# A hybrid mixer layer: another order inside its last stage, four units moved into it, and its check moved to the end

## The chip, the cores and the metric

One core of a Trainium2 chip. The metric is device time in microseconds (us) of one execution of the whole layer, median of several runs. Changes of less than about 0.2% (2.7 us) can't be told from no change here.

## What is computed

One layer over 2048 tokens of width 1024: a conditioned norm of x, a wide projection (1024 to 3600 columns), three mixers on its columns, and an output projection with a residual and a last norm. Everything is in float32; the kernel gets float32 accuracy from TensorE by splitting operands in a high and a low part and summing three products.

```python
h = rms_norm(x) * (1.0 + scale) + shift          # scale, shift, gate from c @ w_ada + b_ada
p = h @ w_in                                     # columns: qa ka va lra ga | qb fb ib gb | qc kc vc gc
log_alpha = log_sigmoid(lra @ w_gla_gate2 + b_gla_gate) / 16
o_a = chunk_gated_linear_attn(qa / 8, ka, va, log_alpha)       # "GLA", 4 heads of 64/128, chunks of 64
log_f = logaddexp(log(lb), log1p(-lb) + log_sigmoid(fb))
o_b = chunk_gated_linear_attn(silu(qb), (1 - lb) * sigmoid(-fb), ib, log_f)   # "HGRN", 4 heads of 64/64
o_c = stick_breaking_attn(qc, kc, vc)            # 4 heads of 64, causal, blocks of 128
o   = [rms_norm(o_a) * gla_norm_w * silu(ga), rms_norm(o_b) * hgrn_norm_w * silu(gb), o_c * silu(gc)]
out = rms_norm(x + gate * (o @ w_out)) * final_norm_w
```

## The kernel before, in words

**Products.** A product in high and low parts is three matmuls (`mm3`, L263 to L266; lines 160 to 162 in `fm_unit`). A **projection unit** (`fm_unit`) makes one block of 128 feature columns for one stretch of 512 tokens: 8 times `mm3`, 24 matmuls of 128x512, summed in one of two PSUM banks (tag `acc` of pool `psA`). Its result leaves by an evacuation on ScalarE (ACT), `ev_act` at L191 or `ev_silu` at L826, and is stored to DRAM. Its weights are loaded and split by `split_w` (L146 load on SP, L147 high part on ACT, L148 low part on VectorE, DVE), in pool `wp` with two buffers each for `wraw`, `whi`, `wlo`. Results pass through pool `stg`, tag `st`, three buffers. Stretches of tokens are taken in the order 3, 2, 1, 0 (`ORDER`); the normed input of a stretch lies in SBUF as `hT[n]` (high and low).

**Stages.** First the norm, the conditioning and the first projections (to about 250 us), then the value columns in token-major units, then eight units for the HGRN forget gate whose evacuation (`ev_forget`, `decay_sums`, L533 to L554, L651 to L661) is a chain over ACT, DVE and GpSimd (POOL). Behind it stands the **flag** (L671 to L686): DVE takes minima of the decay sums in `SM`, TensorE adds up two columns over the partitions (`pf`, L682, in a bank of `psA`), and DVE makes the integer `fi`. At the end of the program `values_load` (L1512) reads it, and a branch runs an exact recurrence, which these inputs don't take. Then comes the **attention stage** (about 475 to 970 us): 80 steps of stick-breaking attention (`sb_stream`) interleaved with 50 projection units (`fill_stream`, `NFILL`), of which five are put ahead (`lead`). In these stages the compiler's list scheduler sets the order of each engine's queue from a simulated time line; each engine's queue is in order.

**Joint stage** (from 970 us, `recurrences_and_projection`). Here the order on TensorE (PE), DVE, ACT and POOL is the program's, written out by hand; SP, which issues the loads and stores, is still ordered by the scheduler. There are 16 steps i: four groups g of 512 tokens, in each the feature pairs 0, 2, 1, 3 (`STEPS`; 0 and 1 are GLA, 2 and 3 HGRN, so odd steps are HGRN). A step does:

- `scores` (PE, L1110) into a pair of banks (tag `two`, two pairs), `causal` (ACT copies them to M, L1116; POOL masks M, L1119)
- `square_sums` of the step before (PE, L1211), from the squares that `evacuate` made on ACT
- `keys` (PE transposes, L1126; ACT copy, L1128), `increments` (PE, L1138, into a pair of banks U), `states` (eight DVE steps in a row, L1147), `decays` of the next step (ACT exponentials, DVE products L1084 to L1092, one POOL product L1091)
- `outputs(i, 1)` and `outputs(i, 0)` (PE, L1168, L1179, into a pair of banks o). Between the two stands an **ordering detour**: PE writes one number (`done`, L1172), ACT copies it (`mark`, L1174), and PE multiplies the mark (L1164) before it goes on
- `evacuate` (ACT copies o to `ots`, L1196, and squares it, L1199; DVE multiplies by norm weight and gate, L1200)
- in odd steps one `attention_block` (k = 6 in steps 1, 5, 9, 13, k = 7 in steps 3, 7, 11, 15): load of the attention's result and gate, DVE product (L1218), ACT high part (L1223), DVE low part (L1224)
- every fourth step, for the group before: `norms` (ACT L1230, L1231; DVE L1233, L1234) and six times `normalise`: PE spreads a row (`bc`, L1238, one bank), DVE multiplies (L1239), ACT high part, DVE low part.

The high and low parts of the finished output go into the SBUF tiles of hT[3] and hT[2], by parity of the group. From step 5 on each step also holds 16 **pieces** `Y` of the output projection (a piece is one `mm3`, L1285 to L1287; eight pieces make half a row tile of 128 tokens, after which DVE adds x, L1290), placed 2+4+2+2+2+3+1 within the step. After the second half `finish` squares on ACT (L1253) and, some pieces later, DVE and POOL make the scale (L77, L78), DVE applies it (L1259) and SP stores. The 64 pieces of the last group follow the last step.

```python
            Y(2, on)
            nrm()
            if i < n:
                if i % 4 == 1:
                    attention_block(i // 4, 6)
                if i % 4 == 3:
                    attention_block(i // 4, 7)
                outputs(i, 1)
            nrm()
            Y(3, on)
            nrm()
            if i < n:
                outputs(i, 0)
                evacuate(i)
            Y(1, on)
```

## Time and profile before

| | us |
|---|---|
| median of 3 runs | 1350.9 (1350.4 to 1352.8) |
| the profiled execution | 1349.0 |
| its span in the trace | 1347.3 |
| PE busy | 1236.2 (92% of the span) |
| DVE, ACT, POOL busy | 677.1, 442.9, 160.2 |
| attention stage, lead units included | about 445 to 970 |
| joint stage | about 970 to 1347 |

The page divides the span in 40 slices of 33.7 us and gives each engine's busy share in tenths, and the TensorE clock that was granted in tenths of full speed. A line of the time line gives start and length of an instruction, and in brackets how long its engine had been idle and what ended that. A line of windows gives, for a stretch, each engine's busy time and instructions, the granted clock, the DMA share and GB/s.

### The profile page before, as it was taken

How to read it: one execution, taken by the hardware profiler on the slowest of the kernel's cores; microseconds unless marked ns; L12 is line 12 of the kernel's file. 1: busy time of each engine (PE TensorE's matmuls, PEld its weight loads, DVE VectorE, ACT ScalarE, POOL GpSimd, SP SyncE). 2: the span in 40 equal slices, each digit the busy share in tenths (PEclk: the TensorE clock that was granted, in tenths of full speed). 3: DMA queues.
4: the chain of work that ended last, by engine and by line, in shares of the span. 5: the costliest groups of instructions: out<-in, count | busy, mean ns of one | idle time of the engine just before them, and what ended most of it. 6: DMA issues, size and time to landing. Idle time of an engine off the chain costs nothing.

```text
span 1347.3 us, 22831 instructions
## 1 busy us (share of the span) xinstructions
PE 1236.2 (92%) x9322; PEld 1001.5 (74%) x9322; DVE 677.1 (50%) x1083; ACT 442.9 (33%) x830; POOL 160.2 (12%) x190
## 2 busy tenths in 40 slices
PE   7999999999994799999999999999775998989996
PEld 6777799999983677777777777777653776767675
DVE  5856316410059473465545665666346445564442
ACT  3375414321144242332333332332233323233211
POOL 3210000000024100100010112111121011111000
PEclk8999999999997899999999999999967799999999
DMA  9775433431134423232242234232354343543221
GB/s 263 223 260 165 148 93 106 138 109 48 55 106 146 133 59 81 89 94 59 81 116 76 74 105 132 83 88 67 101 178 121 93 159 116 154 145 123 75 87 56
DMA packets 153515, 155.17 MB, mean 115 GB/s; under 512 B 30117, under 2 KB 114102, under 8 KB 153402
## 3 DMA queue, kind: packets, MB, share of 16 engines
q1 hardware_dynamic: 124374, 116.39, 29.5%
q10 hardware_dynamic: 29028, 37.24, 7.9%
q8 instruction: 75, 1.23, 0.4%
q14 instruction: 38, 0.31, 0.1%
HBM read 101.16 MB, written 52.43 MB: 114 GB/s over the span
## 4 chain that ended last, share of the span: by engine, by line
PE 71%; DVE 14%; DMA 5%; issue 5%; ACT 4%; SPq 1%; POOL 1%; ACTq 0%; POOLq 0%; DVEq 0%
PE acc L160 8%; PE acc L162 8%; PE acc L161 8%; PE av L788 6%; PE acc L172 5%; PE acc L174 5%; PE acc L173 5%; PE pt L776 4%; PE y L1285 4%; PE y L1286 3%; PE y L1287 3%; PE o L1179 2%; PE o L1168 2%; DMA wg<-in_w_ada_dram 2%; PE acc L266 2%
## 5 line engine op out<-in xcount | busy, mean ns | idle before, releaser
L160 PE MATMUL acc<-hTh,whi 128*128 128x512 f32 x528 | 213.1, 405 | 1.5 <-DVE stl L285 1.0
L162 PE MATMUL acc<-hTh,wlo 128*128 128x512 f32 x528 | 210.0, 398 | 0.0
L161 PE MATMUL acc<-hTl,whi 128*128 128x512 f32 x528 | 208.4, 395 | 0.0
L772 DVE TENSOR_TENSOR_SCAN f<-f 128x512 f32<-128x512 f32 (+3 forms) x160 | 177.0, 1136 | 14.0 <-ACT f L766 6.9
L172 PE MATMUL acc<-whi,hTh 128*128 128x256 f32 (+1 forms) x512 | 146.2, 286 | 1.4 <-ACT stt L199 1.4
L174 PE MATMUL acc<-whi,hTl 128*128 128x256 f32 (+1 forms) x512 | 146.0, 285 | 0.0
L173 PE MATMUL acc<-wlo,hTh 128*128 128x256 f32 (+1 forms) x512 | 145.7, 285 | 0.0
L160 PEld LDWEIGHTS acc<-hTh,whi 128*128 128x128 f32 x528 | 99.9, 189 | 26.2 <-issue 5.1
L162 PEld LDWEIGHTS acc<-hTh,wlo 128*128 128x128 f32 x528 | 99.8, 189 | 23.3 <-issue 2.9
L161 PEld LDWEIGHTS acc<-hTl,whi 128*128 128x128 f32 x528 | 100.0, 189 | 20.0 <-issue 1.4
L1285 PE MATMUL y<-wh,hTh 128*128 128x512 f32 x256 | 108.6, 424 | 0.0
L1286 PE MATMUL y<-wl,hTh 128*128 128x512 f32 x256 | 101.7, 397 | 0.0
L1287 PE MATMUL y<-wh,hTl 128*128 128x512 f32 x256 | 101.3, 396 | 0.0
L766 ACT ACTIVATE f<-zt 128x512 f32<-128x512 f32 (+3 forms) x160 | 81.0, 537 | 58.1 <-DVE f L772 27.2
L172 PEld LDWEIGHTS acc<-whi,hTh 128*128 128x128 f32 x512 | 97.8, 191 | 1.8 <-ACT stt L199 1.6
L173 PEld LDWEIGHTS acc<-wlo,hTh 128*128 128x128 f32 x512 | 97.9, 191 | 0.2
L174 PEld LDWEIGHTS acc<-whi,hTl 128*128 128x128 f32 x512 | 97.8, 191 | 0.0
L788 PE MATMUL av<-PT,V 128*64 128x128 f32 x960 | 90.1, 280 | 1.3 <-DVE PT L781 1.2
L781 DVE COPY PT<-pt 128x512 f32<-128x512 f32 (+1 forms) x80 | 50.3, 628 | 73.5 <-PE pt L776 73.2
L148 DVE TENSOR_TENSOR wlo<-wraw,whi 128x1024 fp32r<-128x1024 f32 (+1 forms) x32 | 39.2, 1229 | 94.4 <-ACT whi L147 82.2
L776 PE MATMUL pt<-ident,f 128*128 128x128 f32 x544 | 84.6, 279 | 1.8 <-DVE f L772 1.4
L788 PEld LDWEIGHTS av<-PT,V 128*64 128x64 f32 x960 | 63.7, 136 | 28.5 <-issue 19.3
(210 smaller groups left out, 1963.0 us busy)
## 6 DMA issues: line engine op xcount, KB each, us to landing
wraw<-in_w_in_dram SPq DMA_DIRECT2D x36, 512.0 KB, 4.8
xt<-in_x_dram SPq DMA_DIRECT2D x16, 512.0 KB, 5.8
wa<-in_w_ada_dram SPq DMA_DIRECT2D x16, 512.0 KB, 6.0
Q<-s_qc SPq DMA_DIRECT2D x64, 128.0 KB, 3.2
s_gate<-sg ACTq DMA_DIRECT2D x32, 256.0 KB, 3.3
gt<-s_gate SPq DMA_DIRECT2D x32, 256.0 KB, 3.9
r<-in_x_dram SPq DMA_DIRECT2D x16, 512.0 KB, 3.6
out_dram<-r SPq DMA_DIRECT2D x16, 512.0 KB, 3.2
```

The costliest lines, as they stand in the source:

```text
L160: mm(ps, hi[:, k, :], th[:, k, :], start=(k == 0), stop=False)
L161: mm(ps, hi[:, k, :], tl[:, k, :], start=False, stop=False)
L162: mm(ps, lo[:, k, :], th[:, k, :], start=False, stop=(k == KT - 1))
L172: mm(o, th[:, k, s], hi[:, k, 0:ncols], start=(k == 0), stop=False)
L173: mm(o, th[:, k, s], lo[:, k, 0:ncols], start=False, stop=False)
L174: mm(o, tl[:, k, s], hi[:, k, 0:ncols], start=False, stop=(k == KT - 1))
L772: nc.vector.tensor_tensor_scan(fr, fr, fr, carry[u], op0=ALU.mult, op1=ALU.bypass)
L776: nc.tensor.transpose(pt[:, b, :], f[:, b * P:(b + 1) * P], ident)
L788: last[0] = mm(av[u * 64:(u + 1) * 64, :], (Dd if diag else V)[J][:, b, :], PT[:, b, :], start=diag, stop=(J == 0 and b == 0))
L1285: mm(y, oh[:, k, us], wh, start=(i == 0), stop=False)
L1286: mm(y, oh[:, k, us], wl, start=False, stop=False)
L1287: mm(y, ol[:, k, us], wh, start=False, stop=(i == KT - 1))
```

## The change

Seven edits. (1) The flag's instructions go into the joint stage as `flag()`, called after the last step's pieces; `pf` now takes a bank of tag `bc`, and `fi` is returned. (2) Four projection units leave the attention stage: of QA, KA and KA+P only two stretches each are made there (before 3, 3 and 4), `NFILL` is 46, and the four units become 32 pieces in steps 0 to 3 of the joint stage (8 ahead of step 0, then 6 a step, `SLOT0`). (3) Within a step `outputs(i, 1)` moves ahead of `keys`; the pieces stand in four stretches (4, 2, 6, 4); the detour (`done`, `mark`) is gone. (4) Both attention blocks come in steps 1, 5, 9, 13. (5) The low parts of `normalise` are made on POOL. (6) Homes: `wp` and `stg` live on through the joint stage; row tiles r use `wraw`/`whi` (four buffers, loaded three ahead), `fnb` and `bsel` use `wlo`; gates, attention results and the squares' junk share `stg`'s three `st` buffers; `ot` has six buffers instead of eight. (7) `finish` makes the scale on ACT (Ln, Exp) right behind the squares, the store follows after five pieces, and the very last row tile is scaled and stored in two halves.

```diff
-NFILL = 50
+NFILL = 46
+SLOT = (4, 2, 6, 4)
+SLOT0 = (2, 1, 2, 1)
...
-    def open_proj_pools():
-        nonlocal psA, wp, stg
-        psA = stA.enter_context(tc.tile_pool(name="psA", bufs=2, space=PSUM))
-        wp = stA.enter_context(tc.tile_pool(name="wp", bufs=2))
-        stg = stA.enter_context(tc.tile_pool(name="stg", bufs=3))
+    psA = stA.enter_context(tc.tile_pool(name="psA", bufs=2, space=PSUM))
+    wp = ctx.enter_context(tc.tile_pool(name="wp", bufs=2, reuse_waits="tile"))
+    stg = ctx.enter_context(tc.tile_pool(name="stg", bufs=3, reuse_waits="tile"))
...
-    pf = psA.tile([1, 2], F32, tag="acc", name="pf")
-    mm(pf, one_col, fl, start=True, stop=True)
...
-    feat_blocks.append((C_QA, ORDER[1:], ev_act((s_feat["qa"][0], AF.Copy, 1.0))))
-    feat_blocks.append((C_KA, ORDER[1:], ev_act((s_feat["ka"][0], AF.Copy, 1.0))))
-    feat_blocks.append((C_KA + P, ORDER, ev_act((s_feat["ka"][1], AF.Copy, 1.0))))
+    feat_blocks.append((C_QA, ORDER[2:], ev_act((s_feat["qa"][0], AF.Copy, 1.0))))
+    feat_blocks.append((C_KA, ORDER[2:], ev_act((s_feat["ka"][0], AF.Copy, 1.0))))
+    feat_blocks.append((C_KA + P, ORDER[2:], ev_act((s_feat["ka"][1], AF.Copy, 1.0))))
...
+    ka1 = split_w(C_KA + P, wp, P, P)
+    qa0 = split_w(C_QA, wp, P, P)
+    left = [(ka1, ORDER[0], ev["ka1"]), (ka1, ORDER[1], ev["ka1"]), (qa0, ORDER[1], ev["qa0"]),
+            (None, ORDER[1], ev["ka0"])]
...
-            else:
-                done = psG.tile([1, 1], F32, tag="sp", name="done")
-                mm(done, t.mark, t.mark, start=True, stop=True)
...
-            if e == 1:
-                done = psG.tile([1, 1], F32, tag="sp", name="done")
-                mm(done, one_col, one_col, start=True, stop=True)
-                t.mark = gq.tile([1, 1], F32, tag="mark", name="mark", bufs=2)
-                nc.scalar.copy(t.mark, done)
-            else:
+            if e == 0:
...
+            pf = psG.tile([1, 2], F32, tag="bc", name="pf")
+            mm(pf, one_col, fl, start=True, stop=True)
...
-            gt = po.tile([P, GTF], F32, tag="gt", name="gt", bufs=2)
+            gt = stg.tile([P, GTF], F32, tag="st", name="gt")
...
-            ots[k] = po.tile([P, GTF], F32, tag="ot", name="ot", bufs=8)
-            nc.sync.dma_start(ots[k], s_o[k][:, g * GTF:(g + 1) * GTF])
-            nc.vector.tensor_tensor(ots[k], ots[k], load_gate(g, k), op=ALU.mult)
-            split_ops(g, k)
+            ot, gt = stg.tile([P, GTF], F32, tag="st", name="oa"), load_gate(g, k)
+            nc.sync.dma_start(ot, s_o[k][:, g * GTF:(g + 1) * GTF])
+            nc.vector.tensor_tensor(ot, ot, gt, op=ALU.mult)
+            split_ops(g, k, ot, nc.vector)
...
-            split_ops(g, k)
+            split_ops(g, k, ots[k], nc.gpsimd)
...
+            nc.scalar.activation(f, f, AF.Ln, bias=eps_col, scale=1.0 / D)
+            nc.scalar.activation(f, f, AF.Exp, scale=-0.5)
...
-            r = pr_.tile([P, D], F32, tag="r", name="r", bufs=3)
+            r = wp.tile([P, D], F32, tag=("wraw", "whi")[u % 2], name="r")
...
+        def units():
+            for i, (w, n, evac) in enumerate(left):
+                ps = psG.tile([P, 512], F32, tag="y", name="acc", bufs=2)
+                if i == 2:
+                    ka0 = split_w(C_KA, wp, P, P)
+                for k in range(KT):
+                    mm3(ps, w or ka0, n, k)
+                    if k == KT - 1:
+                        evac(ps, n)
+                    yield
...
+            Y(i, ya)
+            if live:
+                outputs(i, 1)
+                keys(i)
             nrm()
-            if i < n:
-                keys(i)
-            Y(2, on)
-            nrm()
-            if i < n:
+            Y(i, yb)
+            if live:
                 increments(i)
                 states(i)
                 decays(i + 1)
...
+                    for k in (6, 7):
+                        attention_block(g, k)
                 outputs(i, 0)
                 evacuate(i)
...
+            if i == n:
+                fi = flag()
```

## Rows read from the trace of the kernel before

**Rows 1.** The page, part 2: TensorE's granted clock by slices of 33.7 us.
```profile
PEclk8999999999997899999999999999967799999999
```

**Rows 2.** Windows: stretch, length, busy PE PEld DVE ACT POOL, PEclk, DMA share, GB/s.
```profile
419.50:444.90 25.40, 0.03 (x2) 0.06 (x2) 22.60 (x37) 9.57 (x17) 10.57 (x7) 0.57 0.39 134
444.90:450.30 5.40, 5.40 (x15) 4.25 (x16) 3.21 (x5) 2.75 (x4) 1.18 (x2) 0.50 0.58 149
...
475.20:970.00 494.80, 484.90 (x3029) 374.82 (x3027) 287.43 (x342) 163.67 (x332) 52.82 (x75) 1.00 0.30 85
```

**Rows 3.** Time line around the flag: PE, ACT, DVE.
```profile
444.87 0.19 PE L682 MATMUL pf<-fl,one_col 128*1 128x2 f32 x2 [25.42 <-DVE fl L680]
...
418.15 0.39 PE L162 MATMUL acc<-hTh,wlo 128*128 128x512 f32 x1
...
419.45 0.58 ACT L651 COPY st<-acc 128x512 f32<-128x512 f32 x1 [1.55 <-PE zt L764]
...
427.22 0.58 ACT L651 COPY st<-acc 128x512 f32<-128x512 f32 x1
...
429.07 1.22 DVE L148 TENSOR_TENSOR wlo<-wraw,whi 128x1024 fp32r<-128x1024 f32 x1
...
445.08 1.28 ACT L54 ACT_TABLE_LOAD   x1 [2.73 <-DVE fl L680]
```

**Rows 4.** Time line of ACT: evacuations of two units that PE makes back to back.
```profile
453.29 0.60 ACT L191 ACTIVATE st<-acc 128x512 f32<-128x512 f32 x1 [5.44 <-PE acc L162]
...
458.73 0.60 ACT L191 ACTIVATE st<-acc 128x512 f32<-128x512 f32 x1 [4.84 <-PE acc L162]
```

**Rows 5.** Windows of the joint stage, columns as in Rows 2.
```profile
970.00:977.00 7.00, 0.07 (x11) 0.05 (x10) 1.83 (x4) 2.81 (x4) 0.62 (x1) 0.69 0.96 277
977.00:1054.80 77.80, 52.38 (x903) 40.09 (x907) 39.16 (x77) 24.73 (x48) 13.64 (x16) 0.68 0.47 141
...
1074.10:1093.50 19.40, 19.40 (x254) 14.66 (x233) 7.55 (x15) 4.77 (x11) 2.90 (x4) 1.00 0.47 143
1093.50:1111.50 18.00, 17.36 (x252) 12.61 (x227) 10.27 (x19) 6.13 (x13) 3.23 (x4) 1.00 0.51 168
1111.50:1138.20 26.70, 22.55 (x254) 16.77 (x234) 16.34 (x29) 9.44 (x19) 2.95 (x4) 0.94 0.34 105
...
1273.00:1289.50 16.50, 11.81 (x52) 7.60 (x49) 9.10 (x15) 6.05 (x10) 0.55 (x1) 1.00 0.17 65
...
1030.50:1054.50 24.00, 15.81 (x112) 11.39 (x112) 13.71 (x25) 7.22 (x13) 2.42 (x3) 0.57 0.25 73
```

**Rows 6.** Time line of PE: the detour in steps 1 and 5, and a norm step.
```profile
1002.09 0.18 PE L1164 MATMUL done<-mark 1*1 1x1 f32 x2 [6.06 <-ACT mark L1174]
...
1071.33 0.18 PE L1164 MATMUL done<-mark 1*1 1x1 f32 x2 [0.64 <-ACT mark L1174]
...
1128.05 0.49 PE L1238 MATMUL bc<-rh,bsel 128*128 128x512 f32 x1 [3.39 <-DVE ot L1239]
```

**Rows 7.** Groups of the joint stage by line: count, busy us, mean ns, idle before.
```profile
L1224 DVE TENSOR_TENSOR hTl<-ot,hTh 128x512 fp32r<-128x512 f32 x32 | 22.2, 693 | 21.9 <-ACT hTh L1223 20.5 <-ACT mark L1174 1.4
...
L1196 ACT COPY ot<-o 128x512 f32<-128x512 f32 x24 | 13.3, 588 | 49.8 <-PE o L1179 49.8
```

**Rows 8.** Time line of step 7: DVE's chain to the attention block, POOL's product and mask.
```profile
1102.18 0.28 DVE L1147 SCALAR_TENSOR_TENSOR St<-C,SE,U 128x64 f32<-128x64 f32 x1
...
1105.92 1.42 DVE L1092 TENSOR_TENSOR Qd<-eP,SE 128x512 f32<-128x512 f32 x1
1107.26 0.68 DVE L1218 TENSOR_TENSOR ot<-ot,gt 128x512 f32<-128x512 f32 x1
...
1097.85 1.37 POOL L1119 TENSOR_SCALAR_AFFINE_SELECT M<-M 64x512 f32<-64x512 f32 x2 [14.28 <-ACT M L1116]
...
1105.41 1.37 POOL L1091 TENSOR_TENSOR kt<-bc,SE 128x512 f32<-128x512 f32 x1 [5.55 <-issue]
```

**Rows 9.** DMA issues of the joint stage: KB each, median us from issue to landing.
```profile
gt<-s_gate SPq DMA_DIRECT2D x32, 256.0 KB, 3.9
```

More of the change, by code (lines that the diff above doesn't have):

```diff
@@ L559, in hybrid_mixer_kernel @@
     st0.close()
+    stm = ExitStack()
+    rmask = chunk_mask(stm.enter_context(tc.tile_pool(name="rm", bufs=1, reuse_waits="tile")), GTF)
     st1 = ExitStack()
@@ L1250, in finish @@
         def finish(gr, u, r):
-            fss = pr_.tile([P, 1], F32, tag="fss", name="fss", bufs=2)
-            jk = pr_.tile([P, D], BF16, tag="jk", name="jk")
-            nc.scalar.activation(jk, r, AF.Square, accum_out=fss)
-            def scale():
-                rms_scale(fss)
-            def store():
-                nc.vector.scalar_tensor_tensor(r, r, fss, fnb, op0=ALU.mult, op1=ALU.mult)
-                nc.sync.dma_start(out[0, (4 * gr + u) * P:(4 * gr + u + 1) * P, :], r)
-            later.append([3, scale])
-            later.append([6, store])
+            n = 2 if (gr, u) == (NCH - 1, 3) else 1
+            w = D // n
+            fss = po.tile([P, 2], F32, tag="fss", name="fss", bufs=2)
+            jk = stg.tile([P, D], BF16, tag="st", name="jk")
+            for i in range(n):
+                nc.scalar.activation(jk[:, i * w:(i + 1) * w], r[:, i * w:(i + 1) * w], AF.Square,
+                                     accum_out=fss[:, i:i + 1])
+            f = fss[:, 0:1]
+            if n == 2:
+                nc.vector.tensor_tensor(f, f, fss[:, 1:2], op=ALU.add)
+            nc.scalar.activation(f, f, AF.Ln, bias=eps_col, scale=1.0 / D)
+            nc.scalar.activation(f, f, AF.Exp, scale=-0.5)
+            def store():
+                for i in range(n):
+                    cs = slice(i * w, (i + 1) * w)
+                    nc.vector.scalar_tensor_tensor(r[:, cs], r[:, cs], f, fnb[:, cs], op0=ALU.mult, op1=ALU.mult)
+                    nc.sync.dma_start(out[0, (4 * gr + u) * P:(4 * gr + u + 1) * P, cs], r[:, cs])
+            later.append([5, store])
         def new_r(gr, u):
-            r = pr_.tile([P, D], F32, tag="r", name="r", bufs=3)
+            r = wp.tile([P, D], F32, tag=("wraw", "whi")[u % 2], name="r")
             nc.sync.dma_start(r, x[0, (4 * gr + u) * P:(4 * gr + u + 1) * P, :])
@@ L1293, in projection, with Y @@
                         yield
-        ypieces = projection()
-        def Y(n, active):
-            if active:
-                for _ in range(n):
-                    next(ypieces, None)
-                    tick()
+        def units():
[8 more added lines that the diff above has]
+                    yield
+        fill, ypieces = units(), projection()
+        def Y(i, n):
+            for _ in range(n):
+                if i <= NCH or next(fill, fill) is fill:
+                    if i <= NCH:
+                        next(fill, None)
+                    else:
+                        next(ypieces, None)
+                        tick()
         act_tables("natural_log_exp_and_others")
@@ L1305, in recurrences_and_projection @@
         load(1)
[L1306 to L1309 removed]
         decays(0)
+        Y(0, KT)
         n = len(steps)
         for i in range(n + 1):
[L1313 to L1315 removed]
+            if i == NCH + 1:
+                for _ in fill:
+                    pass
+                t = wp.tile([P, D], F32, tag="wlo", name="fnb")
+                fnb = t
+                nc.sync.dma_start(fnb, fnw.rearrange("(a d) -> a d", a=1).broadcast_to((P, D)))
+            if i == NCH - 1:
+                bself = wp.tile([P, 6, P], F32, tag="wraw", name="bself")
+                nc.sync.dma_start(bself, sel3)
+                bsel = wp.tile([P, 6, P], F32R, tag="wlo", name="bsel")
+                nc.vector.tensor_copy(bsel, bself)
+            ya, yb, yc, yd = SLOT if i > NCH else SLOT0
+            g = i // 4
+            todo = [0, 1, 4, 2, 3, 5] if i % 4 == 0 and i > 0 else []
             def nrm():
                 if todo:
[L1319 to L1321 removed]
+                    normalise(g - 1, todo.pop(0))
+            live = i < n
+            if live:
                 load(i + 2)
```

94 lines of the change are left out of this document (40 added, 54 removed).

## The prediction

> **What bounds the kernel now.** I read the page first, then windows, then the time line of each place where the page shows TensorE (PE) idle. PE is busy 92% of the span, and the granted clock falls below full in the first slices and at two other places, the slices around 420 to 450 us and 975 to 1045 us [rows 1]. Between them PE is the bound: in the attention stage it is busy 484.9 of 494.8 us at full clock [rows 2], so whatever PE work leaves that stage leaves the time. At the first place PE does nothing for 25.4 us, and its own time line names the cause: the flag's matmul at L682 stands at the head of PE's in-order queue and waits for DVE's minima, which come after the whole forget chain [rows 2, 3]. The second place is the start of the joint stage: 7.0 us with almost no work, then 77.8 us with 52.4 us of PE work at a mean clock of 0.68 [rows 5]. Steps 1 and 3 lose 6.06 and about as much again at the detour, since ACT reaches its `mark` copy only behind the attention block [rows 6]; step 4 takes 24.0 us for the norms at clock 0.57 [rows 5]. From step 5 on PE is nearly full: 19.4 us for a GLA step, 18.0 for an HGRN step, and 26.7 for a step with norms, in which PE waits 3.39 us for DVE [rows 5, 6].
>
> **1. The flag moves: -20 (bounds -11 and -28).** Behind the flag stand projection units that need a PSUM bank and split weights. The last two forget units were evacuated at 419.45 + 0.58 and 427.22 + 0.58, and the second block's low weights were ready at 429.07 + 1.22 [rows 3]; the first block's were there before. Without the flag the first unit can start at 420.0, the second at 427.8. What goes is 25.4 us of waiting, and the half-clock stretch behind it, 5.4 us at 0.50 [rows 2], which costs 2.7: together 28.1, the far bound. What stays is 2.4 us before the second unit, plus ACT's lateness in handing banks back: it evacuated the last forget unit at 427.22, 9 us after its last matmul at 418.15 [rows 3]. I charge about 5 us for that, -20.7, and write -20. The near bound: if ACT reaches no evacuation of the new units before its table load at 445.08 [rows 3], only two units go ahead, 2 x 5.44 = 10.9. A unit is 5.44: two units made back to back reach ACT at 453.29 and 458.73 [rows 4].
>
> **2. Four units leave the attention stage: -20 (bounds -18 and -21.8).** 4 x 5.44 = 21.8 in a stage with 2% idle [rows 2, 4]; I keep back 2 us for waits that less PE work uncovers. Three weight blocks are loaded and split once more; DVE's 1.22 each and ACT's copies lie beside PE [rows 3].
>
> **3. Start and first group, 970 to 1054.8, 84.8 us: -7 (bounds -16 and +4).** A piece is an eighth of a unit, 0.68. A later step has 16 pieces, 10.9 us, so an HGRN step keeps 18.0 - 10.9 - 0.64 = 6.5 for the rest and a GLA step 19.4 - 10.9 = 8.5, 7.5 in the mean [rows 4 to 6]. With six pieces (4.1) a step of group 0 is 11.6, four of them 46.4. The eight pieces ahead (5.4) lie over the 7.0 us in which `decays(0)` runs today. Step 1 now holds both attention blocks; I charge it 8 us of waiting (edit 4, with less cover than later). Step 4 has no pieces; its norms lose DVE's low parts, 0.69 each and the like again in waiting for ACT (21.9 us over 32 of them), 6 x 1.37 = 8.2 off 24.0 [rows 5, 7]. 46.4 + 5.4 + 8 + 15.8 = 75.6, and 2 for a clock that still falls in steps 1 and 4: 77.6 against 84.8. The bounds leave out the 8 us, or double it with a clock that stays low.
>
> **4. Steps 5 to 15: +13 (bounds -14 and +28).** Gone: two pairs of one-number matmuls a step, 0.18 a pair [rows 6], some 0.25 once overlap is taken off, 11 steps, -2.7; the 0.64 wait in the odd steps [rows 6], five of them, -2.9. The norm steps 8 and 12: the 3.39 us wait is for the single `bc` bank, which DVE frees after states and decays; in the new order the third spread row still stands behind those, so I take only -1 each, although DVE is lighter. New: **the two attention blocks need four `st` buffers and there are three.** The second gate's load can start only when the first block's product (or its low part) is through, and takes 3.9 us [rows 9]. DVE's chain in program order: it reaches the attention product 5.1 us after the increments (1102.18 to 1107.26), plus 0.68 for a residual add that now stands ahead, plus 0.68 [rows 8]; then 4.3 (the 3.9 and an estimated 0.4 for signal and issue), 0.68 for the second product, 0.62 for the high part on ACT. Only then does ACT copy o, 0.59 [rows 7]: 5.1 + 0.7 + 0.7 + 4.3 + 0.7 + 0.6 + 0.6 = 12.7 us behind the increments. And PE now waits for that copy: with the order scores, o, U on two pairs of banks, the next scores write into the pair that o leaves (before, U's pair, freed long ago). PE is there after six pieces, outputs (an estimate, some 1.8 of the 6.5 above) and four pieces: 4.1 + 1.8 + 2.7 = 8.6. So 4.1 us of idle PE, 5.5 if the freed buffer is the other one; with some loss of clock, as 3.39 us of idle left a mean of 0.94 in step 8 [rows 5, 6], I take +6 in steps 5, 9 and 13, together +18; none if the loads are early enough, 8 each at most. Queued behind the waiting DVE product are the low part, `evacuate` and the residual add, behind SP's waiting load the loads of the step after next, which have more than a step to spare. Last, M must be ready sooner: today the mask ends 5.7 us after the scores start (1093.5 to 1099.22) [rows 5, 8], and the new place needs it after scores, sums (an estimated 2.2 of the same 6.5) and four pieces, some 4.9; the extra ACT scale work adds to it, the earlier o copy takes off. +2, bounds 0 and 6. Sum: -2.7 - 2.9 - 2 + 18 + 2 = +12.4.
>
> The low parts cost POOL some 1.37 each (the nearest row, a POOL product of that size), and DVE loses by it: Qd took 1.42 beside that product, while the next DVE product of the same shape took 0.68 [rows 8]. Six of them in a norm step may cost DVE 6 x 0.74 = 4.4 of the 8.2 it saves. The Trainium skill ("SBUF — State Buffer", section "Who interferes with whom") says the pair of ports that VectorE and GpSimd share is an exclusive lock; the row agrees. It also speaks against the move outright ("GPSIMD Engine Reference", section "Engine selection": elementwise work on VectorE, since GpSimd is about twice as slow with two inputs); by that the saving in norm steps would be nil and the sum 8 us worse in step 4. The sum above does not use either sentence.
>
> **5. Step 16: -3.6.** It takes 16.5 for 16 pieces (10.9) and six spread rows, with PE idle 4.7 [rows 5]. Without DVE's low parts in the way the wait goes but for about 1 us (bounds -1 and -5).
>
> **6. The flag at the end: +2.3 (0 to 3.5).** PE meets `pf` right behind the last piece of step 16 and waits for DVE: a residual add (0.7), four minima, three small operations and the signals, an estimated 1.6 more. The last group's 64 pieces stand behind it. The branch reads `fi` long after.
>
> **7. Last row tile: -1 (0 to -2).** Halved scale and store; ACT's two small operations replace one on DVE and one on POOL.
>
> **Sum.** -20 - 20 - 7 + 12.4 - 3.6 + 2.3 - 1 = -36.9. The profiled execution took 1349.0, its span 1347.3; the median of the runs, 1350.9, lies 1.9 above it. 1350.9 - 36.9 = **1314**.
>
> **Rivals.** *A, the attention loads don't stop PE.* For it: no product of an attention block waits for its loads today. Against: four tiles on three buffers. Then the +18 and most of step 1's 8 are gone: 1314 - 25 = 1289. *B, the flag's gap is filled with another wait.* The scheduler may put attention matmuls, which need the sigmoid table (loaded at 445.08 [rows 3]), ahead of units whose bank comes late, and PE would idle there instead. For it: the same queue did so with the flag. Against: units have the earlier place in the program. Then term 1 is -2 to -11: 1323 to 1332. *C, slower: every joint step gets a new wait, at `outputs(i, 1)` for M or at the scores for o's copy.* What is saved without new waits is 57 us; over 17 steps that is 3.4 us a step. The point from which it decides: if PE idles about 2.5 us in each step, as it did in group 0, its clock drops too, to a mean of 0.68 there [rows 5], and 10.9 us of pieces take 16. That is 5 + 2.5 a step from step 5 on, and some 3 in group 0: 1350.9 - 57 + 12 x 7.5 + 15 = 1399. Against: from step 5 on four pieces stand ahead of both places. *D, the change doesn't do what it says:* the units stretch group 0 by their full 21.8, since PE is not idle where they stand. Then term 3 is +15: 1336.
>
> **Chances.** Forecast 0.70 (1298 to 1334), A 0.15, B 0.07, C 0.04, D 0.04. Range: 1288 to 1335, which takes in A and most of B. Faster by over 0.2% 0.94, within 0.2% 0.02, slower 0.04 (0.2%, 2.7 us, is about what a measurement can tell from no change).
>
> **What would show it.** Right: no PE idle over 10 us between 419 and 450; the attention stage ending near 930; a first group of about 78 us; in steps 1, 5, 9 and 13 a PE wait of 4 to 6 us at the scores, ended by ACT's copy of o, and a DVE wait for a gate's load just before. Wrong: waits of that kind in the even steps (C), no such wait at all (A), a gap before the attention transposes at 430 to 448 (B). The forecast fails most easily on the +18 of edit 4, which no row shows, and on ACT's place for the first evacuations.

## The result, and the profile after

| | before | after |
|---|---|---|
| median, us | 1351.6 (4 runs, 1350.4 to 1352.8) | 1390.5 (4 runs, 1388.7 to 1391.9) |
| ratio | | 1.0287, interval 1.0268 to 1.0306 |
| profiled execution, its span | 1349.0, 1347.3 | 1391.9, 1390.1 |
| PE, DVE, ACT, POOL busy | 1236.2, 677.1, 442.9, 160.2 | 1260.7, 656.9, 506.6, 184.0 |

The change made the kernel 39 us slower; 37 faster was forecast. The span by stages shows where. The boundaries are the first and the last product `av` of the attention stage and the first zeroing product of `scores` in a step. "Tied" is the first experiment below: the kernel after with one edit more.

| stretch, us | before | after | tied | forecast change | tied minus before |
|---|---|---|---|---|---|
| to the first `av` | 477.6 | 460.6 | 461.0 | -20 | -16.6 |
| first to last `av` | 492.3 | 481.4 | 478.6 | -20 | -13.7 |
| from there to step 5 | 84.6 | 93.9 | 88.8 | -7 | +4.2 |
| steps 5 to 14 | 202.3 | 253.7 | 212.9 | +12.4 | +10.6 |
| step 15 to the last product | 80.3 | 89.1 | 78.4 | -2.3 | -1.9 |
| behind it | 10.2 | 11.4 | 9.0 | (in the row above) | -1.2 |

The table is made from the profiled executions: before's took 2.6 us less than the median of its runs, after's 1.4 more, and tied's (1330.4) 3.8 less.

The first two stretches are shorter, as meant. The loss is in the joint stage, and most of it in steps 5 to 14. First the page's row of the granted clock, which answers to [rows 1]: full where the flag's gap was, and below 0.9 in seven of the last twelve slices, which are the joint stage.

```profile
PEclk9999999999999999999999999999869988988998
```

The windows of the kernel after answer to [rows 2, 5]: the stretch in which the flag's gap lay, the first group, then steps 6, 7 and 8. Columns as there.

```profile
418.30:453.00 34.70, 29.19 (x123) 22.86 (x124) 27.03 (x38) 16.56 (x27) 12.85 (x10) 1.00 0.57 173
...
942.00:1035.90 93.90, 75.20 (x961) 53.16 (x960) 39.37 (x85) 34.21 (x56) 19.22 (x21) 0.79 0.53 159
...
1054.30:1082.40 28.10, 20.98 (x219) 16.16 (x218) 9.76 (x18) 10.27 (x17) 2.99 (x3) 0.94 0.37 116
1082.40:1103.80 21.40, 18.70 (x221) 13.74 (x221) 8.45 (x16) 7.65 (x12) 3.21 (x3) 0.92 0.42 124
1103.80:1137.90 34.10, 25.60 (x225) 18.58 (x224) 13.02 (x23) 16.07 (x24) 8.57 (x8) 0.85 0.31 92
```

A GLA step takes 28.1 us where it took 19.4, an HGRN step 21.4 for 18.0, a norm step 34.1 for 26.7 [rows 5]. PE idles 7.1, 2.7 and 8.5 us in the last three rows (length less busy time), where it idled 0, 0.6 and 4.2, and ACT has twice the work of before in the GLA step, 10.27 us for 4.77 [rows 5]. The time line of step 6 says what ACT does (first PE at the sums of squares, then ACT, POOL, PE at `outputs(i, 1)`):

```profile
1058.42 1.04 PE L1207 MATMUL ss<-sq,sel 128*32 128x512 f32 x2 [3.28 <-ACT sq L1195]
...
1059.85 1.06 ACT L1253 ACTIVATE jk<-r 128x1024 bf16<-128x1024 f32 x1 [1.47 <-DVE r L1294]
...
1061.02 1.28 ACT L1258 ACT_TABLE_LOAD   x1
1062.31 0.29 ACT L1258 ACTIVATE fss<-fss,eps_col 128x1 f32<-128x1 f32 x1
1062.62 1.28 ACT L1259 ACT_TABLE_LOAD   x1
1063.92 0.20 ACT L1259 ACTIVATE fss<-fss 128x1 f32<-128x1 f32 x1
1064.03 0.57 ACT L1100 COPY M<-sc 128x512 f32<-128x512 f32 x1
...
1064.66 2.01 POOL L1103 TENSOR_SCALAR_AFFINE_SELECT M<-M 64x512 f32<-64x512 f32 x2 [14.43 <-ACT M L1100]
...
1066.01 0.43 PE L1149 MATMUL o<-M,Vn 64*128 64x64 f32 x2 [3.55 <-POOL M L1103]
```

`finish` now makes its scale on ACT with Ln (L1258) and Exp (L1259), and each of the two reloads ACT's function table, 1.28 us. Both stand ahead of the copy of M, POOL masks M behind that copy, and PE waits 3.55 us for it; the two loads take 2.56 us (in the tied kernel, which has neither, the same wait is 1.01). The first wait, 3.28 us, is another thing (below). The groups of ACT's table loads, by line (count, busy us, mean ns): 48 in all, where the kernel before has 6.

```profile
L1258 ACT ACT_TABLE_LOAD x16 | 20.5, 1283 | 0.3
L1259 ACT ACT_TABLE_LOAD x16 | 20.5, 1283 | 0.3
L1226 ACT ACT_TABLE_LOAD x4 | 5.1, 1283 | 0.1
L1227 ACT ACT_TABLE_LOAD x4 | 5.1, 1283 | 0.1
```

The kernel has a load for this: L56, which brings the table that holds Ln and Exp together, asked for ahead of the joint stage. ACT's time line at the end of the attention stage shows what became of it:

```profile
936.61 1.04 ACT L143 CAST whi<-wraw 128x1024 fp32r<-128x1024 f32 x1 [5.58 <-PE acc L157]
937.67 1.28 ACT L56 ACT_TABLE_LOAD   x1
938.96 0.27 ACT L772 COPY ost<-av 128x128 f32<-128x128 f32 x1
939.25 1.28 ACT L806 ACT_TABLE_LOAD   x1
...
940.54 0.60 ACT L806 ACTIVATE sg<-acc 128x512 f32<-128x512 f32 x1
...
943.78 1.28 ACT L1066 ACT_TABLE_LOAD   x1 [1.17 <-issue]
```

It runs at 937.67, **ahead of the last gate's sigmoid**, which puts the sigmoid table back at 939.25. From then on the joint table isn't brought in again: the first Exp behind it, at L1066, gets a load, and so do the Ln and the Exp of every later pair. In the kernel before the load stood behind every sigmoid:

```profile
971.75 1.28 ACT L54 ACT_TABLE_LOAD   x1 [1.16 <-issue]
```

Why it moved is read from the program and the time line, and was not tried by itself. The load is asked for by `act_tables`, and it seems to keep its place only behind the ACT instruction written last ahead of it. Before, that belonged to the attention stage. The change puts `split_w` for `ka1` and `qa0` between the two, and the load follows their copies (the last, at 936.61, stands right ahead of it) while one sigmoid is still to come. That the loads behind this misplaced one are what costs the time is the theory, T. The rival, R: the new order inside a step (M needed sooner, the norms' rows elsewhere) makes PE wait, and the loads only fill ACT beside it.

### The profile page after: what moved, and what is told of

It reads as the page before. It is cut to its first block, busy times and chain, and to the rows that moved or that the text cites. A ratio compares the mean times of both kernels' runs of the same rounds, so it can differ in the third digit from the quotient of the medians.

```text
span 1390.1 us, 22712 instructions
## 1 busy us (share of the span) xinstructions
PE 1260.7 (91%) x9258; PEld 1011.6 (73%) x9258; DVE 656.9 (47%) x1048; ACT 506.6 (36%) x893; POOL 184.0 (13%) x198
## 5 line engine op out<-in xcount | busy, mean ns | idle before, releaser
L156 PE MATMUL acc<-hTh,whi 128*128 128x512 f32 x496 | 200.2, 405 | 7.1 <-ACT st L649 3.2
L158 PE MATMUL acc<-hTh,wlo 128*128 128x512 f32 x496 | 196.3, 396 | 0.0
L157 PE MATMUL acc<-hTl,whi 128*128 128x512 f32 x496 | 195.0, 393 | 0.0
L752 DVE TENSOR_TENSOR_SCAN f<-f 128x512 f32<-128x512 f32 (+3 forms) x160 | 170.8, 1099 | 15.4 <-ACT f L746 7.1
L156 PEld LDWEIGHTS acc<-hTh,whi 128*128 128x128 f32 x496 | 93.4, 188 | 32.7 <-issue 5.1
L158 PEld LDWEIGHTS acc<-hTh,wlo 128*128 128x128 f32 x496 | 93.4, 188 | 22.2 <-issue 3.1
L157 PEld LDWEIGHTS acc<-hTl,whi 128*128 128x128 f32 x496 | 93.6, 189 | 18.2 <-issue 1.0
L1290 PE MATMUL y<-wl,hTh 128*128 128x512 f32 x256 | 106.6, 416 | 0.0
L1291 PE MATMUL y<-wh,hTl 128*128 128x512 f32 x256 | 106.3, 415 | 0.0
L746 ACT ACTIVATE f<-zt 128x512 f32<-128x512 f32 (+3 forms) x160 | 81.1, 539 | 54.1 <-DVE f L752 21.9
L768 PEld LDWEIGHTS av<-PT,V 128*64 128x64 f32 x960 | 65.0, 138 | 27.8 <-issue 16.9
L748 POOL TENSOR_SCALAR_AFFINE_SELECT f<-f 128x128 f32<-128x128 f32 x64 | 31.1, 491 | 390.5 <-ACT f L746 367.1
```

The source lines that it names most:

```text
L156: mm(ps, hi[:, k, :], th[:, k, :], start=(k == 0), stop=False)
L157: mm(ps, hi[:, k, :], tl[:, k, :], start=False, stop=False)
L158: mm(ps, lo[:, k, :], th[:, k, :], start=False, stop=(k == KT - 1))
L752: nc.vector.tensor_tensor_scan(fr, fr, fr, carry[u], op0=ALU.mult, op1=ALU.bypass)
L768: last[0] = mm(av[u * 64:(u + 1) * 64, :], (Dd if diag else V)[J][:, b, :], PT[:, b, :], start=diag, stop=(J == 0 and b == 0))
L1290: mm(y, oh[:, k, us], wl, start=False, stop=False)
```

## The experiments

The kernel before was measured again beside each set of runs: 1350.1 us beside e1 to e4, 1350.2 beside e5 to e8, 1352.4 beside e9 to e12. Differences between the last set and the others are uncertain by these 2 us.

**The table load tied behind the sigmoids (e1_pin).** The kernel after, with the load tied to the last sigmoid of the gates and to the last of the attention stage, which `sigm` holds:

```diff
-        act_tables("natural_log_exp_and_others")
+        with tc.issue_after(sigm["gate"].ins), tc.issue_after(sigm["attn"].ins):
+            act_tables("natural_log_exp_and_others")
```

> The kernel after, with one edit: the load of the ScalarE table that holds Ln and Exp together is tied behind the last sigmoid of the gates and of the attention stage, as it in fact fell in the kernel before (971.7 us, the last of 6 loads in the trace). In the kernel after it falls at 937.7 us, a sigmoid at 939.2 us replaces it, and some 40 loads of 1.28 us follow, two for each Ln and Exp pair. Theory T (these loads keep ScalarE from the copies of M and from the norms, and TensorE waits for those): the loads go from about 44 to about 6, each joint step after step 4 loses 2 to 7 us, and the time is 1335 to 1350 us. What stays of the waits then is the stall of the attention blocks, about 3 us in each of steps 2, 6, 10, 14. Rival R (the new places of outputs(i, 1) and of the norm steps make TensorE wait by themselves, and the loads lie beside other work): the loads go as well, but the time stays within 10 us of 1390.

1334.3 us (1330.4 to 1337.8), 0.9891 of before (0.9874 to 0.9908). 6 table loads are left, and 56 us are gone by the medians: T holds. In the table above 40.8 us go in steps 5 to 14. Windows of these steps, after and tied:

```profile
1035.90:1289.60 253.70, 210.33 (x2203) 155.06 (x2202) 96.22 (x174) 95.96 (x151) 46.78 (x44) 0.89 0.34 105
```
```profile
1028.40:1241.30 212.90, 191.05 (x2208) 141.67 (x2209) 96.42 (x174) 67.56 (x129) 46.77 (x44) 0.96 0.41 125
```

PE's idle time falls from 43.4 to 21.9 us, about half of the 40.8. The other half is PE's own work, which takes 19.3 us less at a granted clock of 0.96 for 0.89. So the 42 loads, 53.9 us on ACT, don't simply add up to the 56: half of the price is waiting, and half is the lower clock of the stretch in which PE waits.

In step 4 of the first group, which takes 24.3 us, two long waits stay. They stand at the third and the sixth spread row, for the one bank that DVE's product of the row before has to free:

```profile
1016.13 0.80 PE L1235 MATMUL bc<-rh,bsel 128*128 128x512 f32 x1 [4.65 <-DVE ot L1236]
...
1027.68 0.79 PE L1235 MATMUL bc<-rh,bsel 128*128 128x512 f32 x1 [3.14 <-DVE ot L1236]
```

**The finished row's scale back on DVE and POOL (e2_finish).** The kernel after, the misplaced load left as it is, and

```diff
-            nc.scalar.activation(f, f, AF.Ln, bias=eps_col, scale=1.0 / D)
-            nc.scalar.activation(f, f, AF.Exp, scale=-0.5)
+            def scale():
+                rms_scale(f)
...
+            later.append([3, scale])
             later.append([5, store])
```

> The kernel after, with the scale of a finished row tile back on VectorE and GpSimd as in the kernel before (three pieces later), so that 16 of the Ln and Exp pairs on ScalarE are gone; the four pairs of the norms and the place of the first table load stay. Theory T (table loads): 32 of some 44 loads go, at 1.28 us each 41 us of ScalarE time, and the time falls to 1350 to 1365 us; the steps 4, 8 and 12, which carry the norms' own pairs, change least. Rival R (the new order within a step): nothing of the order changes, so 1380 to 1390 us. If VectorE and not ScalarE is what is late, this run is slower than 1390 us, as it gives VectorE more to do.

1345.3 us (0.9962, 0.9948 to 0.9977). 32 loads fewer, 45 us; the eight of the norms and two more stay. Better than expected, since Ln and Exp on ACT cost something even without the loads (e10_fin). R is out as the cause of the loss.

**The flag alone (e3_flag).** The kernel before with edit 1.

```diff
-    pf = psA.tile([1, 2], F32, tag="acc", name="pf")
...
+            if i == n:
+                fi = flag()
```

> The kernel before, with one part of the change alone: the flag's reductions, its one small product and its comparison stand at the end of the joint stage instead of ahead of the attention stage. The gap of 25.4 us on TensorE ahead of the flag's product goes but for the waits that the trace of after still shows there (1.5, 1.6, 1.5 and 0.8 us), and at the end the product of the flag waits 1.9 us: 1326 to 1332 us if nothing gives it back. If the attention stage is bound by something else than TensorE's work (its transfers, or the throttle), which the 7 us instead of 20 us of after would speak for, it gives back up to 13 us: 1337 to 1345 us.

1336.5 us (0.9899, 0.9883 to 0.9916), between the two ranges. The first `av` comes at 458.2 for 477.6, **-19.4**; the attention stage takes 493.1 for 492.3 and gives next to nothing back. What does is the end: from step 15 on 83.6 us for 80.3, since PE waits there for the flag:

```profile
1276.98 0.19 PE L1182 MATMUL pf<-fl,one_col 128*1 128x2 f32 x2 [2.95 <-DVE fl L1180]
```

**The order alone (e4_order).** The kernel before with edit 3: `outputs(i, 1)` ahead of `keys`, pieces in 4, 2, 6, 2 and 2, and no detour.

```diff
+                outputs(i, 1)
                 keys(i)
...
-                done = psG.tile([1, 1], F32, tag="sp", name="done")
-                mm(done, t.mark, t.mark, start=True, stop=True)
```

> The kernel before, with one part of the change alone: the order within a joint step (outputs(i, 1) ahead of keys, pieces of the projection in four stretches of 4, 2, 6 and 2) and no detour of a product over ScalarE between outputs(i, 1) and outputs(i, 0). Units, attention blocks, flag, norms' homes and the table load stay as before. Theory T (the order is sound, and M is late only where table loads stand ahead of its copy): 1340 to 1352 us, the gain being the detour's waits, about 0.5 us in a step. Rival R (with outputs(i, 1) ahead of keys TensorE waits 2 us for M in each of 12 steps by the order alone): 1365 to 1385 us.

1349.8 us, ratio 0.9995 (0.9986 to 1.0005): no difference. In its trace steps 5 to 14 take 199.9 for 202.3 and the rest from step 15 on 77.7 for 80.3, as the waits at the detour are gone, but the first group takes 90.2 for 84.6, and the norm steps 8 and 12 take 28.3 and 28.1 for 26.7 and 26.4. Half of the 6 us that PE lost at the detour in steps 1 and 3 [rows 6] turns up at the next product that needs ACT, the sums of squares (step 2; step 4 has 3.00 too):

```profile
1005.74 1.91 PE L1203 MATMUL ss<-sq,sel 128*32 128x512 f32 x2 [3.00 <-ACT sq L1191]
```

**The attention blocks split again (e5_split).** The kernel of e1_pin, edit 4 undone.

```diff
-                if i % 4 == 1:
-                    for k in (6, 7):
-                        attention_block(g, k)
+                if i % 4 == 1:
+                    attention_block(g, 6)
+                if i % 4 == 3:
+                    attention_block(g, 7)
```

> The kernel of the first experiment (table load tied behind the sigmoids), with the attention blocks split again as in the kernel before: block 6 in the steps 1, 5, 9, 13 and block 7 in the steps 3, 7, 11, 15. In that kernel's trace steps 2, 6, 10 and 14 take 23.4, 23.9, 24.8 and 25.0 us, with waits of 9.3, 3.2, 3.0 and 3.4 us at the sums of squares; the second block's load is sent only after the first block's product (972.6 us), lands at 978.1, and ScalarE copies its high part before it copies o. Theory B (the pair of blocks is what holds ScalarE): steps 6, 10, 14 fall to about 19.4 us as in the kernel before and step 2 to 12 to 14, together 25 us, less what a block costs in its new step, 0 to 3 us in each of steps 4, 8, 12 and 16: 1310 to 1322 us. Rival S (these steps are long for the work that stands in them, and the waits for o come with outputs(i, 0) late in the step): 1328 to 1336 us.

1323.5 us (1321.7 to 1325.1): 10.8 less than e1_pin. Steps 6, 10, 14 fall from 23.9, 24.8 and 25.0 to 19.4, 19.4 and 19.3, step 2 from 23.4 to 17.1, while steps 4, 8 and 12 grow by 5.4, 1.6 and 1.6. The mechanism stands in e1_pin's time line of step 1 (SP, DVE, ACT, then PE in step 2):

```profile
971.86 0.68 DVE L1215 TENSOR_TENSOR oa<-oa,gt 128x512 f32<-128x512 f32 x1
...
972.57 0.32 SPq L1214 DMA_DIRECT2D oa<-s_o  x1
...
978.18 0.69 DVE L1215 TENSOR_TENSOR oa<-oa,gt 128x512 f32<-128x512 f32 x1 [4.26 <-DMA oa<-s_o]
...
978.91 0.62 ACT L1220 CAST hTh<-oa 128x512 fp32r<-128x512 f32 x1 [5.72 <-DVE oa L1215]
979.43 0.58 ACT L1193 COPY ot<-o 128x512 f32<-128x512 f32 x1
980.04 0.63 ACT L1196 ACTIVATE sq<-ot 128x512 f32<-128x512 f32 x1
...
980.72 1.91 PE L1208 MATMUL ss<-sq,sel 128*32 128x512 f32 x2 [9.34 <-ACT sq L1196]
```

The second block's load goes out only when the first product has freed its buffer, and the copy of o queues on ACT behind the second block's high part.

**A fourth buffer instead (e6_buf4).** The kernel of e1_pin, both blocks in one step, and

```diff
-            ot, gt = stg.tile([P, GTF], F32, tag="st", name="oa"), load_gate(g, k)
+            gt = load_gate(g, k)
+            ot = po.tile([P, GTF], F32, tag="oa", name="oa") if k == 7 else stg.tile([P, GTF], F32, tag="st", name="oa")
```

> The kernel of the first experiment with a fourth buffer for the two attention blocks: o of block 7 has one of its own, and both blocks stay in one step. Theory B1 (the missing fourth buffer makes the second load late, as the prediction had it): both loads go out at once, ScalarE has both copies done before o is ready, and the time is 1312 to 1322 us, as with the blocks split. Theory B2 (what counts is that the copies of two blocks stand on ScalarE ahead of o's copy, wherever their data lie): the sums of squares still wait 2 to 3 us in steps 6, 10 and 14, and the time is 1326 to 1334 us.

1325.6 us (1323.1 to 1326.7): 8.6 of the 10.8. The two products now follow within 2 us (1044.62 and 1046.59 in step 5), and the wait at the sums falls from 3.16 to 0.68:

```profile
1049.13 1.04 PE L1208 MATMUL ss<-sq,sel 128*32 128x512 f32 x2 [0.68 <-ACT sq L1196]
```

The time lies between the ranges of B1 and B2, and so does the trace. Steps 6, 10 and 14 take 21.7, 22.9 and 21.3 us, where they took 23.9, 24.8 and 25.0, and 19.4 with the blocks split: the fourth buffer gives about half of what the pair costs there. With it, PE waits 1.0 to 1.3 us for M at `outputs(i, 1)` in these steps, which it doesn't with the blocks split. So the missing buffer is half of it (B1), and the work of two blocks on ACT in one step the other half (B2). The total is nearer to e5_split than that, since step 4 takes 26.1 us here and 29.7 there.

**The low parts back on DVE (e7_low).** The kernel of e1_pin, edit 5 undone.

```diff
-            split_ops(g, k, ots[k], nc.gpsimd)
+            split_ops(g, k, ots[k], nc.vector)
```

> The kernel of the first experiment with the norms' low parts on VectorE again, as in the kernel before. The prediction took the subtraction on GpSimd at 1.37 us against 0.69 on VectorE and set 2 us in each of steps 8, 12 and 16 for the move as a gain. If that holds, undoing it gives 1338 to 1342 us. If the low parts on GpSimd stand in the way of the masks of M, or slow VectorE beside them, undoing it gives 1326 to 1331 us. Within 2 us of 1334 if both cancel.

1343.4 us (1342.0 to 1344.4), 9.1 more: the move to POOL was worth 9 us. The traces don't show a wait that it took away. Step 8 takes 26.1 us in e1_pin and 28.0 here, with 3.1 us more work on DVE, but PE idles 5.3 us in it there and 5.5 here, and e5_split and e8_units, with the low parts on POOL, take 27.8 at a clock of 0.94 too. Step 8, then the whole joint stage, e1_pin ahead of e7_low each time:

```profile
1087.70:1113.80 26.10, 20.79 (x225) 15.48 (x224) 13.07 (x23) 10.80 (x20) 8.52 (x8) 1.00 0.40 118
```
```profile
1094.00:1122.00 28.00, 22.51 (x230) 16.26 (x229) 16.18 (x28) 10.29 (x19) 2.36 (x3) 0.94 0.31 95
```
```profile
939.60:1319.70 380.10, 334.87 (x3628) 248.89 (x3626) 161.44 (x296) 115.62 (x220) 75.79 (x72) 0.94 0.40 123
```
```profile
941.50:1332.50 391.00, 345.87 (x3626) 254.76 (x3626) 175.85 (x319) 115.63 (x220) 44.88 (x48) 0.91 0.40 120
```

Over the joint stage PE idles 45 us in both. The 10.9 us between them lie in PE's busy time, at a granted clock of 0.94 and 0.91. How the low parts' place comes to that is not shown.

**The units back in the attention stage (e8_units).** The kernel of e1_pin, edit 2 undone.

```diff
-NFILL = 46
+NFILL = 50
...
+    left = []
```

> The kernel of the first experiment with the four units back in the attention stage, so that the first group of the joint stage has no other work to fill with. The prediction set -20 us for the attention stage and -7 us for the first group, 27 in all: by it this run takes 1361 us. The traces say less: from the first product of the attention stage to its last 492.3 us before, 478.6 in the kernel of the first experiment, and from there to step 5 84.6 and 88.8 us: 1343 to 1346 us if the first group then takes what it took before. If the first group loses more than that without the units, its wait at step 2 being none of theirs, 1326 to 1336 us.

1347.3 us (1344.7 to 1352.9), just above the 1343 to 1346 that the traces gave: moving the units was worth 13 us, not 27. Windows of its attention stage and first group, then the same of e1_pin:

```profile
458.30:952.90 494.60, 484.79 (x3020) 374.75 (x3019) 287.36 (x342) 162.21 (x330) 52.72 (x75) 1.00 0.30 87
952.90:1043.10 90.20, 59.33 (x859) 44.12 (x858) 38.29 (x75) 28.38 (x49) 19.80 (x21) 0.59 0.47 136
```
```profile
461.00:939.60 478.60, 464.92 (x2914) 356.80 (x2914) 283.00 (x340) 160.69 (x325) 50.82 (x75) 0.99 0.30 87
939.60:1028.40 88.80, 68.64 (x956) 48.54 (x955) 39.84 (x79) 30.24 (x53) 19.40 (x21) 0.85 0.56 171
```

PE's work in the attention stage falls by 19.9 us, its idle time grows from 9.8 to 13.7, and the stage starts 2.7 later, as the first `av` now waits 3.49 us for DVE's copy of PT where e3_flag, with the units, shows no such wait: 19.9 - 3.9 - 2.7 = 13.3. In the first group the four units cost nothing: 88.8 with them, 90.2 without.

**Two spread rows moved (e9_nrm).** The kernel of e5_split, and

```diff
             Y(i, yb)
+            nrm()
             if live:
                 increments(i)
                 states(i)
                 decays(i + 1)
-            nrm()
...
+            nrm()
             if live:
...
                 outputs(i, 0)
                 evacuate(i)
-            nrm()
```

> The kernel with the table load tied and the attention blocks split (1323.5 us), with two of the norm steps' spread rows moved: the second goes ahead of increments and states instead of behind them, the fifth ahead of outputs(i, 0) and evacuate instead of behind them. In its trace step 8 waits 3.26 us for the bank of the third row, since VectorE's product of the second stands behind the eight state operations and decays (1100.0 us, the row was spread at 1095.6), and 2.05 us for the bank of the sixth, since the fifth's product stands behind evacuate's. Theory N (the place in VectorE's queue is the wait): both waits go in steps 4, 8 and 12, and the norm steps lose 4 to 5 us each: 1308 to 1315 us. Rival (VectorE or ScalarE has no room, and the wait goes to the next row or to the copy of o): the norm steps stay at 27 to 28 us, 1320 to 1325 us.

1314.1 us (1311.8 to 1317.0), 9.4 less than e5_split and in N's range; steps 4, 8 and 12 take 27.0, 23.0 and 24.2 for 29.7, 27.8 and 27.6. Not all of it goes: in step 8 the fourth row now waits 2.47, and step 5 takes 21.1 for 18.8, as PE waits 2.12 for DVE at its sums of squares. PE's wait in e5_split, then in this kernel:

```profile
1100.72 0.73 PE L1235 MATMUL bc<-rh,bsel 128*128 128x512 f32 x1 [3.26 <-DVE ot L1236]
...
1112.48 0.50 PE L1235 MATMUL bc<-rh,bsel 128*128 128x512 f32 x1 [2.05 <-DVE ot L1236]
```
```profile
1101.36 0.50 PE L1235 MATMUL bc<-rh,bsel 128*128 128x512 f32 x1 [2.47 <-DVE ot L1236]
```

**The scale's home without table loads (e10_fin).** The kernel of e5_split with the edit of e2_finish.

> The kernel with the table load tied and the attention blocks split, with the scale of a finished row tile back on VectorE and GpSimd, as in the kernel before. This is the home that the second experiment tried with the table loads still there. With the loads gone the two small operations on ScalarE take 0.29 and 0.20 us beside TensorE's work. If the change of home is worth nothing by itself (as the prediction had it: its -1 was for the last row tile), 1321 to 1326 us. If VectorE is the engine that is late in the norm steps, as undoing the low parts showed (9 us for 24 operations of 0.69), 1326 to 1332 us.

1318.1 us (1315.4 to 1319.2): 5.4 less, outside both expectations; more work for DVE did not make the kernel slower. Every step without norms is 0.5 us shorter (16.8 for 17.3, 18.9 for 19.4). In step 11 of e5_split the Ln and Exp of `finish` still stand ahead of the copy of M, and PE waits a little for the mask; here the same product runs through. ACT and PE of e5_split, then PE of this kernel:

```profile
1153.03 0.29 ACT L1259 ACTIVATE fss<-fss,eps_col 128x1 f32<-128x1 f32 x1
1153.35 0.20 ACT L1260 ACTIVATE fss<-fss 128x1 f32<-128x1 f32 x1
1153.46 0.57 ACT L1101 COPY M<-sc 128x512 f32<-128x512 f32 x1
...
1156.17 0.68 PE L1150 MATMUL o<-M,Vn 64*64 64x64 f32 x14 [0.21 <-POOL M L1104]
```
```profile
1152.11 0.68 PE L1150 MATMUL o<-M,Vn 64*64 64x64 f32 x16
```

**The sums of squares later (e11_ss).** The kernel of e9_nrm; the flag's DVE part one step earlier; in steps without norms

```diff
-            square_sums(i - 1)
             Y(i, ya)
             if live:
                 outputs(i, 1)
                 keys(i)
+            square_sums(i - 1)
```

> The kernel of run e9_nrm, with the flag's reductions one step earlier (its product stays), and the square sums of steps without norms moved behind outputs(i, 1) and keys. The flag's wait of 1.9 us should go. On the sums: if the 3.0 us that TensorE waits there in step 2 are lost only by the place, 3 us go in the first group; if the first group is bound by the chain over ScalarE (copy of o, square, copy of M), the wait turns up at outputs(i, 1) or at the next product, and nothing is won. 2 us below e9_nrm by the second, 5 to 6 below it by the first.

1323.4 us (1321.6 to 1324.4), 9.3 **more** than e9_nrm, worse than both. The sums, about 1.2 us of PE, had covered the time until M is masked. Where they come later, every step without norms waits at `outputs(i, 1)`: step 7, shown here, is 1.2 us longer (18.5 for 17.3). The flag's wait went as expected. In step 2 the 3.00 us at the sums became 2.71 at `outputs(i, 1)`: what holds step 2 is the chain over ACT, wherever PE meets it.

```profile
1075.39 0.33 PE L1150 MATMUL o<-M,Vn 64*64 64x64 f32 x2 [0.76 <-POOL M L1104]
1076.11 0.68 PE L1150 MATMUL o<-M,Vn 64*64 64x64 f32 x14 [0.40 <-POOL M L1104]
```

**Six pieces moved into step 4 (e12_spread).** The kernel of e9_nrm, the flag's DVE part one step earlier, and

```diff
-SLOT0 = (2, 1, 2, 1)
+SLOT0 = ((2, 1, 1, 1), (2, 1, 1, 1), (2, 1, 2, 1), (1, 1, 0, 0), (1, 2, 3, 2))
```

> The kernel of run e9_nrm, with the flag's reductions one step earlier, and six of the 32 pieces of the four units moved from steps 0, 1 and 3 into step 4, where TensorE waits some 11 us in all for the norms. If pieces in steps 0, 1 and 3 are on the path there (those steps show no wait of TensorE) and fill a wait in step 4, 4 us go: with the flag's 2 some 6 below e9_nrm. If steps 0, 1 and 3 are held by ScalarE's chain and only show no wait because the pieces fill it, new waits stand in them, and the time is 2 us below e9_nrm or above that.

1311.0 us (1308.1 to 1313.2), ratio to before 0.9699 (0.9675 to 0.9723): the best of the runs, 3.0% faster than before and 5.7% than after. 3.1 less than e9_nrm, with ranges that overlap, and between the two expectations: the flag's wait is gone (from step 15 on 76.4 for 78.4), the first group takes 81.0 for 85.1, and steps 5 to 14 give 2.4 back.

## Why the prediction was wrong

**What failed: a step that is missing.** The prediction listed ACT's Ln and Exp in part 7 as two small operations that replace one on DVE and one on POOL, and priced the whole at -1 for the last row tile. It counted the three weight blocks of edit 2 as work beside PE and didn't ask what else their place in the program moves. The price was the place of the table load: +56 us by e1_pin. The time of such a load, 1.28 us, stood in [rows 3], and the call that asks for it in the printed function; the question that was not put is which instruction holds it there. Rival C had the place right, PE waiting for M at `outputs(i, 1)`, but not the cause: with the loads gone steps 7, 9, 11 and 13 show no wait there above 0.25 us. That its sum (1399) came near 1390.5 is luck. It priced 2.5 us of idle PE in a step with a clock of 0.68, as in group 0; but group 0 idled 25.4 us in five steps [rows 5], and step 7 of the kernel after, with 2.7 us idle, ran at 0.92.

**The terms, read with the loads gone.** The median is then 1334.3 for a forecast of 1314. By the profiled spans the saving is 18.6 us for 36.9, so 18.3 are missing:

1. *Flag, -20:* right; -19.4 alone.
2. *Units leave, -20:* mis-sized. By e8_units the four units are 19.9 us of PE work there, not 21.8, and instead of the 2 us kept back 6.6 us of waits come up that they had covered; the term is -13.3. Against before, it is -10.9: the attention stage ends 30.3 us sooner, 19.4 of it the flag's.
3. *First group, -7:* failed, +4.2. The pieces cost what was forecast: steps 0, 1 and 3 take 12.0, 11.4 and 10.6 us for 11.6, and the group takes 90.2 without the units (e8_units), so they are hidden and rival D falls. Two steps failed. Step 2 takes 23.4 for 19.6, the 8 us for the two blocks included; PE waits 9.34 in it, and 3.00 with the blocks split. Step 4 takes 24.3 for 15.8. The prediction took 8.2 us off it for the low parts, as if all that DVE is spared came off PE's time; by e7_low it is 2.2. PE still idles 10.2 us in it, most of it at the third and the sixth spread row, whose bank DVE frees only behind the states and behind `evacuate` (shown at e1_pin above); with the low parts on DVE it idles 10.1. Splitting the blocks shortens step 2 and not the group, which takes 87.9 for 88.8, as step 4 grows by 5.4.
4. *Steps 5 to 15, +12.4:* +10.6 for steps 5 to 14, right in sum by luck, since the parts miss and cancel. In these ten steps the two blocks in one step cost 11.7 us (e5_split) for +18, M and the scale on ACT 6.0 (e10_fin) for +2, the order gives 2.4 (e4_order) for 5.6, and the low parts 5.1 (e7_low) for 2, together +10.2. The 5.6 has a slip: five waits of 0.64 are 3.2 and not 2.9, and from step 5 to 15 there are six odd steps.
   - *The blocks.* The four tiles on three buffers, which no row of before showed, are a real cost, but only about half of the 4.5 to 5.7 us that the pair of blocks costs in each of steps 6, 10 and 14 (e6_buf4). The late load was taken too short: in e1_pin's step 1 it is 5.6 us from the freed buffer to the second product, for 4.3. And the place was wrong: PE meets the late ACT at the sums of squares, one product on from the scores.
   - *The low parts.* The prediction cited a rule against the move from the Trainium skill ("GPSIMD Engine Reference", section "Engine selection": about twice as slow with two inputs). The ratio is borne out: in e1_pin's trace POOL takes 1.28 us for such a low part, in e7_low's DVE takes 0.69. The kernel is faster with them on POOL all the same, and the measurement decides. Nor does the feared loss on DVE show: in step 8 the move spares DVE 3.1 of six times 0.69 us, so about 1 us is lost there, an estimate from the two windows of e7_low's section, and not 4.4.
5. *Step 16 and 6, the flag at the end, with 7:* -3.1 for -2.3 (-1.9 up to the last product, -1.2 behind it). PE waits for the flag 2.95 us in e3_flag, 1.88 in the kernel after and in e1_pin.

The account: the loads +56; of the 18.3 that are missing, term 3 is off by 11 and term 2 by 9, and the others nearly cancel.

**What stays open.** The first group runs at a granted clock between 0.57 (e4_order) and 0.89 (e12_spread). PE idles 30.9 of 90.2 us in it in e8_units, 20.2 of 88.8 in e1_pin and 12.4 of 81.0 in e12_spread; what the clock alone would give back no run separated. That the place of the load is the cause was tried (e1_pin). That the weight blocks moved it was not: e3_flag and e4_order, which leave them out, keep their 6 loads, but no run has the blocks alone.

## What to carry to other kernels

Before work is put between two stages, look for instructions that hold a state for the next one (a function table, a mask, a mode) and for what keeps them in place; tie them to the last user of the old state by name. An engine that is busy a third of the time still sets the pace if the one copy that the busiest engine waits for stands behind its new work: count what stands ahead of that copy. Work taken off an engine is not yet time taken off the kernel: in step 4 of the first group 8.2 us were forecast for it, and 2.2 came. Work that seems to fill an engine can be the cover of a wait (units, sums of squares); ask what is late next when it goes.

## What was not expected of the hardware

A pair Ln and Exp reloaded the table twice where the load of the joint table had been displaced. The Trainium skill ("ScalarE: Activation LUTs", section "Table sets: the hidden batching unit") counts one load for such a pair, as one set holds both; here the 40 loads at L1226 to L1259 are two for each of 20 pairs, and there is none at these places where the joint set was brought in by hand and stayed (e1_pin). A switch took 1.28 us with the next instruction 0.01 us behind it (1061.02 + 1.28, 1062.31).
